# Output rows of two heads of a gated linear attention layer: transposed by DMA in 16-bit words instead of by TensorE

## The chip, the cores and the metric

The kernel runs on one core of a Trainium2 chip, in one launch. The metric is the device time of one execution in microseconds (us). The engines are TensorE (PE in the profile; its weight loads are PEld), VectorE (DVE), ScalarE (ACT), GpSimd (POOL), and SyncE (SP), which here does nothing but issue DMAs. ACT also issues some DMAs on a queue of its own.

## The reference

Two layers run over 528 tokens, 16 learned meta tokens and 512 others: first gated linear attention (GLA) with four heads, then differential softmax attention, with a root mean square norm before each and one at the end. The change is in the first. Its core, cut:

```python
def gla_branch(xn, w_in, w_gate_up, b_gate, gnorm, w_out):      # xn: 528 x 1024
    q, k, v, z, g_lr = split(xn @ w_in)                          # four heads: q, k 256 wide, v, z 512 wide
    lg = log_sigmoid(g_lr @ w_gate_up + b_gate) / 16
    ...                                                          # o = causal, decayed linear attention of q, k, v
    o = o * rsqrt(mean(o * o, axis=-1) + 1e-6) * gnorm           # for each head and token, over 512 values
    y = silu(z) * o
    return y @ w_out
```

Everything is float32, and the kernel keeps nearly that precision: each operand of a product is split into a rounded high part and a remainder (fp32r), and the product is made of three.

## The kernel before

**Layout.** Channels lie on the 128 partitions and tokens in the free dimension, for the projections and for z. Within a head the tokens are cut into block 0 (the 16 meta tokens) and blocks 1 to 4 of 128 each (`BLK`). The output o of a block comes out of TensorE with tokens on the partitions, 128 x 512, since the norm runs over a token's 512 values; y is wanted with channels on the partitions, 4 x 128 channels by tokens, as operand of the output projection. So every block's output has to be turned.

**The steps round the change.** `gla_blocks` (L1194) runs once a head. For each block `output` makes o in a PSUM tile `ps` (L371 are its products), ACT squares it and sums the squares (L1215), DVE and POOL make the reciprocal root (L512, L513), and ACT copies o, scaled by it, to an SBUF tile `t` (L1217), taken from five buffers (`tmp`). `rows` of a block is called after the fill that follows `output`: TensorE transposes the four 128 x 128 pieces by products with an identity (L1239), DVE multiplies them by z out of PSUM (L1241), and `split` makes the high part on ACT (L269) and the remainder on DVE (L270). The rows of block b-1 stand just ahead of the output of block b, those of block 4 at the end.

**What sets the order.** TensorE's program is in the order in which the code is written. Between the steps of a head, `W.fill(us)` draws products from queued generators: projections of the following head and the output projection of the head before. They go through three kinds of PSUM bank, bx, by and bv (L402), each of them in groups of four or eight products of 264 columns, whose results ACT and DVE take up in partial sums (ACT copies one bank to `u` at L423, DVE adds at L448). `fill=(1.9, 1.6)` are the microseconds of such products ahead of and behind each block; block 0 has 0.6 ahead. ACT, DVE, POOL and SP get their order from a scheduler, in which the steps marked `@urgent` go ahead of others. Behind `gla_blocks` the generators are run dry (`W.finish`), and the next head begins with its z, its scores, and `gla_cross` for four blocks (products at L1176, copies of them to `cm` on ACT, L378 and L379, called from `gla_ready`) beside the value projection of the head after it. The output projection of a head (products at L938) runs in the next head's stretch.

**Weights and queues.** Weight halves are loaded by SP into `raw` (two buffers), ACT makes the high part `wh` (L269), DVE the remainder `wl` (L270); for sums of two weights DVE adds first (L337). A generator asks for the next one when it has used one up. SP's queue also carries, late in each head, a conditional copy of scores (`steep`, L1160).

**Turning by DMA** exists for the values of heads 1 and 2 (and of the second layer): `turn_by_dma` (L549) has ACT copy a 32-bit tile so that the low and high 16-bit words of each number lie apart (L560, 128 x 1056 words to `keep`), writes it to DRAM on ACT's queue (L561), and reads it back on SP's by a transposing DMA of 16-bit words (L569), which puts the words together again with rows and columns changed. `W.follow(steps)` queues steps that come when so many microseconds of products have been drawn, `behind` holds transposing DMAs until SP has issued its next weight load, and `W.land()`, ahead of `gla_blocks`, makes sure that all is done. Head 3 makes its values by TensorE during head 2.

Of the kernel before, what the change touches and what calls it, by code (L numbers as in the profile page):

```python
# [20 lines left out]
P = 128  # L21
# [52 lines left out]
class Weaver:  # L74
# [17 lines left out]

    def follow(self, *steps):

        self.away.append([steps[0][0], list(steps)])

    def onward(self, us=0.0):
        for d in list(self.away):
            d[0] -= us
            while d[0] <= 0:  # L100
                d[1].pop(0)[1]()
                if not d[1]:
                    self.away.remove(d)
                    break
                d[0] += d[1][0][0]

    def land(self):

        while self.away or self.behind:
            self.onward(1000.0)  # L110
            while self.behind:
                self.behind.pop(0)()

# [95 lines left out]
def trunk(ctx, tc, x, meta, g_norm, gla_w_in, gla_w_gate_up, gla_b_gate, gla_gnorm, gla_w_out,  # L209
# [21 lines left out]
    def T(p, shape, dt, tag, **kw):  # L231
        uid[0] += 1
        return p.tile(shape, dt, tag=tag, name=f"{tag}_{uid[0]}", **kw)
# [58 lines left out]
    def load(key):  # L292
        t = load_w(*key) if len(key) == 4 else load_blocks(*key)
        while behind:
            behind.pop(0)()
        return t
# [252 lines left out]
    def turn_by_dma(planes, groups, ends, us, done, last):  # L549
# [7 lines left out]
        @urgent  # L557
        def leave(m, src):
            pl = words(planes[:, m, :]).rearrange("p (h c) -> p h c", h=2)
            act.activation(pl, words(src).rearrange("p (c h) -> p h c", h=2), AF.Copy)  # L560
            act.dma_start(vd[m], pl)  # L561
            left.remove(m)
            if not left:
                W.follow((4.0, lambda: behind.append(turn)))

# [359 lines left out]
    def q_gla_out(hd, s, sink=None):  # L925
# [3 lines left out]
        def gen():  # L929
            turns[0] = 0  # L930
            for c in range(4):
                h = ws.take()
# [260 lines left out]

    def gla_blocks(hd, s, fill, last):  # L1194

# [6 lines left out]
        def output(b):  # L1202
# [14 lines left out]
            act.activation(on[:n], po[:n], AF.Copy, scale=st[:n, 1:2])  # L1217
            return on

        def take_y():  # L1220
# [24 lines left out]

        prev = None
        for b in range(5):
            W.fill(fill[0] if b else 0.6)
            if prev is not None:
                rows(b - 1, prev)  # L1250
            prev = output(b)
            W.fill(fill[1])
        W.fill(2.0)
        rows(4, prev)

# [17 lines left out]
    for hd in range(G_HEADS):  # L1273
# [32 lines left out]
        W.land()  # L1306
        gla_blocks(hd, s, (1.2, 1.2) if last else (1.9, 1.6), last)
        W.finish()
# [575 lines left out]
```

## Time and profile before

| | before |
|---|---|
| three runs: median (lowest to highest) | 986.19 us (986.02 to 986.84) |
| the profiled execution, its time | 986.58 us |
| its span in the trace | 984.8 us |
| TensorE busy | 969.7 us, 98% |
| DVE, ACT, POOL busy | 777.3, 615.6, 50.7 us |
| TensorE clock granted, mean | 0.997 of full speed |
| the two stretches of `gla_blocks` of heads 1 and 2 | from 212 and 316 us on |

The span runs from the first to the last instruction in the trace, and the execution's time has some 2 us round it. In the profile each group of instructions has its line, engine, operation, and its tiles as out<-in. A row of a timeline gives the start, the length in us, engine, line, operation, tiles, shapes and how many alike follow each other, with the idle time before it and what released it in brackets. Lengths of TensorE's instructions are modelled and overlap; distances between starts do not. Groups are made of instructions of one line; L402, for instance, is the line of all projection products.

### The profile page before, as it was taken

Reading aid. Unit: us, or ns where it says so; the run is one execution under the profiler, and the core shown is the slowest. Engines: PE = TensorE matmul, PEld = TensorE weight load, DVE = VectorE, ACT = ScalarE, POOL = GpSimd, SP = SyncE. Lnnn points to the kernel's source line nnn. Section 1 sums busy time; section 2 is a strip of 40 time slices with the busy share of each in tenths; the row PEclk is TensorE's granted clock in tenths of the full one; section 3 lists DMA queues with packets and bytes.
Section 4 is the critical chain, followed back from the end, with each engine's and each line's share of the span. In section 5 each row is a group of like instructions: output and inputs, shape, how many; then the busy total and the mean of one; then the engine's idle time right before and its main releaser. Section 6 shows DMA issues by size and latency. Waiting matters only on the chain. (4 is left out here: it accounts for less than half of the span.)

```text
span 984.8 us, 18186 instructions
## 1 busy us (share of the span) xinstructions
PE 969.7 (98%) x7065; PEld 915.2 (93%) x7065; DVE 777.3 (79%) x1584; ACT 615.6 (63%) x1306; POOL 50.7 (5%) x68
## 2 busy tenths in 40 slices
PE   8999999999999999999999999999999999999997
PEld 8999999999999999999999998898998999988896
DVE  7889985987687888556998885877968879677785
ACT  7776755566546666536657675566764667654583
POOL 1000000000000100000000101001010000000001
PEclk9999999999999999999999999999999999999999
DMA  7322223731363322122332524335353351622222
GB/s 194 87 74 74 74 87 127 143 87 44 111 158 87 86 73 76 68 86 87 97 87 77 149 63 137 83 98 135 86 147 86 97 135 49 184 60 81 86 65 86
DMA packets 150474, 96.27 MB, mean 98 GB/s; under 512 B 33117, under 2 KB 136829, under 8 KB 150384
## 3 DMA queue, kind: packets, MB, share of 16 engines
q1 hardware_dynamic: 147504, 89.61, 33.5%
q10 hardware_dynamic: 2880, 5.46, 1.6%
q8 instruction: 57, 0.93, 0.4%
q14 instruction: 33, 0.27, 0.1%
HBM read 83.64 MB, written 7.57 MB: 93 GB/s over the span
## 5 line engine op out<-in xcount | busy, mean ns | idle before, releaser
L270 DVE TENSOR_TENSOR wl<-raw,wh 128x1024 fp32r<-128x1024 f32 x98 | 119.6, 1222 | 26.9 <-ACT wh L269 19.9
L269 ACT ACTIVATE wh<-raw 128x1024 fp32r<-128x1024 f32 x98 | 103.0, 1053 | 52.2 <-PE by L938 26.6
L402 PE MATMUL bv<-x,wh 128*128 128x264 f32 (+1 forms) x656 | 97.7, 287 | 0.8 <-DVE t L448 0.6
L402 PE MATMUL bx<-x,wh 128*128 128x264 f32 (+1 forms) x640 | 95.1, 286 | 0.2
L402 PEld LDWEIGHTS bv<-x,wh 128*128 128x128 f32 x656 | 86.3, 189 | 1.8 <-DVE t L448 1.5
L402 PEld LDWEIGHTS bx<-x,wh 128*128 128x128 f32 x640 | 84.6, 188 | 1.4 <-ACT u L423 0.6
L392 PE MATMUL bx<-x,wh 128*128 128x512 f32 (+1 forms) x256 | 62.5, 386 | 0.0
L423 ACT ACTIVATE u<-bx 128x264 f32<-128x264 f32 (+1 forms) x120 | 45.4, 379 | 24.1 <-PE bx L402 21.9
L270 DVE TENSOR_TENSOR wl<-sum,wh 128x1024 fp32r<-128x1024 f32 x41 | 50.1, 1221 | 11.0 <-ACT wh L269 9.7
L1618 ACT ACTIVATE p<-p,st 128x528 f32<-128x528 f32 (+3 forms) x64 | 36.4, 569 | 31.7 <-DVE st L1616 31.4
L402 PE MATMUL bv<-x,wl 128*128 128x264 f32 (+1 forms) x328 | 55.2, 285 | 0.1
L1654 POOL TENSOR_TENSOR st<-st,mhalf 128x1 f32<-128x1 f32 x32 | 30.6, 957 | 466.4 <-ACT on L1652 422.8
L402 PE MATMUL bx<-x,wl 128*128 128x264 f32 (+1 forms) x320 | 53.8, 285 | 0.0
L392 PEld LDWEIGHTS bx<-x,wh 128*128 128x128 f32 x256 | 44.5, 188 | 8.0
L269 ACT ACTIVATE wh<-sum 128x1024 fp32r<-128x1024 f32 x41 | 43.3, 1055 | 10.7 <-PE bv L402 4.0
L269 ACT ACTIVATE a11h<-raw 128x512 fp32r<-128x512 f32 x41 | 25.7, 628 | 35.5 <-DMA raw<-in_diff_w_in_dram 18.0
L402 PE MATMUL by<-x,a12h 128*128 128x264 f32 (+1 forms) x320 | 46.7, 286 | 0.2 <-DVE t L448 0.2
L402 PE MATMUL bx<-x,a11h 128*128 128x264 f32 (+1 forms) x320 | 46.5, 285 | 0.0
L402 PEld LDWEIGHTS bv<-x,wl 128*128 128x128 f32 x328 | 45.9, 188 | 0.4 <-issue 0.3
L402 PEld LDWEIGHTS bx<-x,wl 128*128 128x128 f32 x320 | 45.0, 188 | 0.5 <-DVE wl L270 0.2
L402 PEld LDWEIGHTS bx<-x,a11h 128*128 128x128 f32 x320 | 42.3, 188 | 0.8
L402 PEld LDWEIGHTS by<-x,a12h 128*128 128x128 f32 x320 | 41.7, 188 | 0.6 <-DVE t L448 0.4
(479 smaller groups left out, 2644.2 us busy)
## 6 DMA issues: line engine op xcount, KB each, us to landing
raw<-in_gla_w_in_dram SPq DMA_DIRECT2D x48, 512.0 KB, 4.2
raw<-in_diff_w_in_dram SPq DMA_DIRECT2D x42, 512.0 KB, 5.6
raw<-in_diff_w_in_dram SPq DMA_DIRECT2D x11, 1024.0 KB, 5.7
raw<-in_gla_w_out_dram SPq DMA_DIRECT2D x8, 1024.0 KB, 5.3
raw<-in_diff_w_out_dram SPq DMA_DIRECT2D x8, 1024.0 KB
vd<-planes ACTq DMA_DIRECT2D x12, 268.0 KB, 3.0
vd<-keep ACTq DMA_DIRECT2D x8, 264.0 KB, 2.3
T<-bdr SPq DMA_DIRECT2D x8, 264.0 KB, 3.6
```

The lines of the kernel that those rows point to most:

```text
L269: act.activation(hi, src, AF.Copy)
L270: dve.tensor_tensor(lo, src, hi.bitcast(F32), op=ALU.subtract)
L392: pe.matmul(bank, a[:, k, :], b[k] if n0 is None else b[k][:, n0 + i * nn:n0 + (i + 1) * nn], start=n == 0 and ks[0] == 0, stop=n == len(t ...
L402: pe.matmul(bank[:, :x[q].shape[2]], w[p][:, k * P:(k + 1) * P], x[q][:, k, :], start=first and i == 0, stop=i == len(PASSES) - 1, skip_gr ...
L423: W.moved = act.activation(t, self.bx[:, :self.n], AF.Copy, scale=self.sc)
L1618: act.activation(p[:, :nk], p[:, :nk], AF.Exp, scale=-1.0, bias=st[:, m:m + 1], accum_out=st[:, 2 + m:3 + m])
L1654: pool.tensor_tensor(ms, ms, mhalf[:, :1], op=ALU.pow)
```

## The change

For heads 1 and 2 (`far`) the outputs of blocks 1 to 4 are turned by transposing DMAs in place of TensorE. For each block ACT copies the scaled output, words of its numbers apart, to a tile of its own (128 x 1024 words) and starts the write to DRAM on its queue. After each pair of blocks, (1, 2) and (3, 4), one transposing DMA on SP's queue (issued behind the next weight load, or at the latest when the head's output projection begins) brings both back into the first four of the eight rows of `b_all`, an SBUF buffer of the gates that is free then and takes the word copies of the next head's values after, with channels on the partitions. `scaled_rows` of each block follows 11.0 and 1.5 us of drawn products later: the multiply by z in DVE, now in SBUF and in place, and `split` as before. Block 0 keeps TensorE. `fill` becomes (0.6, 1.2) in these heads, the fill of 2.0 and the rows behind block 4 are gone, and `W.land(s)` at the start of the head's output projection makes the queued steps of that head come. Heads 0 and 3 are as before.

```diff
--- before.py
+++ after.py
@@ -90,12 +90,12 @@
     def defer(self, us, fn):
         self.late.append([us, fn])
 
-    def follow(self, *steps):
-
-        self.away.append([steps[0][0], list(steps)])
-
-    def onward(self, us=0.0):
-        for d in list(self.away):
+    def follow(self, *steps, tag=None):
+
+        self.away.append([steps[0][0], list(steps), tag])
+
+    def onward(self, us=0.0, tag=None):
+        for d in [d for d in self.away if tag in (None, d[2])]:
             d[0] -= us
             while d[0] <= 0:
                 d[1].pop(0)[1]()
@@ -104,12 +104,13 @@
                     break
                 d[0] += d[1][0][0]
 
-    def land(self):
-
-        while self.away or self.behind:
-            self.onward(1000.0)
-            while self.behind:
-                self.behind.pop(0)()
+    def land(self, tag=None):
+
+        while any(tag in (None, d[-1]) for d in self.away + self.behind):
+            self.onward(1000.0, tag)
+            for d in [d for d in self.behind if tag in (None, d[-1])]:
+                self.behind.remove(d)
+                d[0]()
 
     def spent(self, us):
         self.onward(us)
@@ -292,7 +293,7 @@
     def load(key):
         t = load_w(*key) if len(key) == 4 else load_blocks(*key)
         while behind:
-            behind.pop(0)()
+            behind.pop(0)[0]()
         return t
 
     def w_pair(shape):
@@ -561,7 +562,7 @@
             act.dma_start(vd[m], pl)
             left.remove(m)
             if not left:
-                W.follow((4.0, lambda: behind.append(turn)))
+                W.follow((4.0, lambda: behind.append((turn, None))))
 
         def turn():
             for blocks, c0 in groups:
@@ -928,6 +929,7 @@
 
         def gen():
             turns[0] = 0
+            W.land(s)
             for c in range(4):
                 h = ws.take()
                 for mm in range(2):
@@ -1191,7 +1193,7 @@
             gla_cross(hd, s, b)
             W.fill(1.5)
 
-    def gla_blocks(hd, s, fill, last):
+    def gla_blocks(hd, s, fill, last, far):
 
         s.y = None
 
@@ -1217,6 +1219,37 @@
             act.activation(on[:n], po[:n], AF.Copy, scale=st[:n, 1:2])
             return on
 
+        def far_rows(pair):
+
+            yd = T(dp, [2, P, 2, 512], U16, "yd", bufs=2)
+            src = yd.rearrange("m p h c -> (m p h) c")
+            i = pair[0] - 1
+            raw = b_all[:, i:i + 2, :].rearrange("p m c -> p (m c)")[:, :8 * P].rearrange("p (m c) -> p m c", m=4)
+            left = [0, 1]
+
+            @urgent
+            def leave(j, on):
+                pl = words(tmp()[:, :512]).rearrange("p (h c) -> p h c", h=2)
+                act.activation(pl, words(on).rearrange("p (c h) -> p h c", h=2), AF.Copy)
+                act.dma_start(yd[j], pl)
+                left.remove(j)
+                if not left:
+                    W.follow((4.0, lambda: behind.append((turn, s))), tag=s)
+
+            def turn():
+                tc.keep_in_program_order(sp.dma_start(words(raw), src, transpose=True))
+                W.follow((11.0, lambda: scaled_rows(0)), (1.5, lambda: scaled_rows(1)), tag=s)
+
+            def scaled_rows(j):
+                t0, n = BLK[pair[j]]
+                y = raw[:, :, j * P:(j + 1) * P]
+                with tc.issue_after(W.mark.ins):
+                    dve.tensor_tensor(y, y, s.z[:, :, t0:t0 + n], op=ALU.mult)
+                    for m0, m1, hi, lo in s.groups:
+                        split(hi[:, :, t0:t0 + n], lo[:, :, t0:t0 + n], y[:, m0:m1, :])
+
+            return leave
+
         def take_y():
 
             if not last:
@@ -1243,15 +1276,20 @@
             for m0, m1, hi, lo in s.groups:
                 split(hi[:, :, t0:t0 + n], lo[:, :, t0:t0 + n], y[:, m0:m1, :n])
 
-        prev = None
+        prev, leave = None, None
         for b in range(5):
             W.fill(fill[0] if b else 0.6)
-            if prev is not None:
+            if prev is not None and (b == 1 or not far):
                 rows(b - 1, prev)
             prev = output(b)
+            if far and b:
+                if b % 2:
+                    leave = far_rows((b, b + 1))
+                leave(1 - b % 2, prev)
             W.fill(fill[1])
-        W.fill(2.0)
-        rows(4, prev)
+        if not far:
+            W.fill(2.0)
+            rows(4, prev)
 
     W.fill(5.0)
     pf = ps_tile()
@@ -1304,7 +1342,8 @@
         else:
             W.stop = q_gla_v(hd + 1, heads[hd + 1])
         W.land()
-        gla_blocks(hd, s, (1.2, 1.2) if last else (1.9, 1.6), last)
+        far = hd in (1, 2)
+        gla_blocks(hd, s, (1.2, 1.2) if last else (0.6, 1.2) if far else (1.9, 1.6), last, far)
         W.finish()
         W.stop = None
 
```

Three pieces of the engines' orders follow, before and after. Numbers behind names tell tiles apart and shift between the two versions, as lines do by one to five behind the edits (to L1217) and by more behind `far_rows` (the transposes are L1272 in place of L1239).

TensorE in `gla_blocks` of head 1, ahead of and at block 1's output; by, bv and bx are banks of the projection that fills, ident,t the transposes of the 16 meta rows, and ps_5617 and ps_5588 the output of block 1. Before:

```order
L402 MATMUL by_5564<-x_2_78,a12l_5455 128x264 x4
L402 MATMUL bv_5582<-x_4_80,wh_5450 128x264 x8
L402 MATMUL bv_5582<-x_4_80,wl_5451 128x264 x4
L402 MATMUL bx_5473<-x_752_3925,wh_5519 128x264 x3
L1239 MATMUL ps_5608<-ident,t_5550 128x16 x4
L371 MATMUL ps_5617<-v_885_4661,a_905_4759 128x512
```

After:

```order
L403 MATMUL by_5564<-x_2_78,a12h_5454 128x264 x8
L403 MATMUL by_5564<-x_2_78,a12l_5455 128x264 x4
L1272 MATMUL ps_5579<-ident,t_5550 128x16 x4
L372 MATMUL ps_5588<-v_885_4661,a_905_4759 128x512
L372 MATMUL ps_5588<-v_886_4662,a_905_4759 128x512
```

Eight, four and three products that stood ahead of the meta rows' transposes are behind block 1's output now.

ACT in the stretch of head 1 in which head 2's values are projected beside `gla_cross`; raw_5716 and raw_5758 are the same weight and wh_6072 and wh_6058 its high part, keep_83 the word copies of head 2's values that the kernel had before, cm copies of cross products, of which those from ps_6117 before and ps_6103 after belong to block 2. Before:

```order
L269 ACTIVATE a_1110_5986<-t_5998 128x512
L560 ACTIVATE keep_83<-t_5960 128x1056
L269 ACTIVATE wh_6072<-raw_5716 128x1024
L561 DMA vd_5540<-keep_83 128x1056
L560 ACTIVATE keep_83<-t_5959 128x1056
L378 ACTIVATE cm_6088<-ps_6091 32x128
```

After:

```order
L379 ACTIVATE cm_6074<-ps_6077 32x128
L562 DMA vd_5540<-keep_83 128x1056
L380 ACTIVATE cm_6074<-ps_6077 32x128
L424 ACTIVATE u_6094<-bx_6014 128x264
L379 ACTIVATE cm_6074<-ps_6103 32x128
L380 ACTIVATE cm_6074<-ps_6103 32x128
L270 ACTIVATE wh_6058<-raw_5758 128x1024
```

The high part stood ahead of all cm copies and stands behind those of blocks 1 and 2 now.

DVE in the same stretch of head 2, where head 3's values are projected and TensorE turns them itself; t_7235 and t_7210 are value columns, sum_7360 the sum for a weight that is used later, keep_83,z the multiply by z of the rows that came back by DMA, and y their remainder. Before:

```order
L270 TENSOR_TENSOR a11l_7357<-raw_7228,a11h_7356 128x512
L337 TENSOR_TENSOR sum_7360<-raw_7228 128x512
L337 TENSOR_TENSOR sum_7360<-sum_7360,raw_7228 128x512
L381 TENSOR_TENSOR am_7269<-t_7273,am_7269 32x16
L448 SCALAR_TENSOR_TENSOR t_7235<-by_7318,u_7300 128x264
```

After:

```order
L1247 TENSOR_TENSOR keep_83<-keep_83,z_6546 128x4x128
L449 SCALAR_TENSOR_TENSOR t_7210<-bv_7212,u_7278 128x264
L271 TENSOR_TENSOR y_1237_6844<-keep_83,y_1236_6843 128x4x128 x2
L271 TENSOR_TENSOR wl_7229<-sum_7163,wh_7228 128x1024
L449 SCALAR_TENSOR_TENSOR t_7210<-by_7296,u_7278 128x264
```

The sum and the remainder a11l that stood ahead of the value columns are further down now, and the multiply of the turned rows and their remainders stand there.

## The prediction

> **What bounds the kernel now.** I read the busy table of the page first, then the waits, then TensorE's instructions in order of time round the edited stretch, then what ACT, DVE, POOL and SP do in it.
>
> ```profile
> span 984.8 us, 18186 instructions
> PE 969.7 (98%) x7065; PEld 915.2 (93%) x7065; DVE 777.3 (79%) x1584; ACT 615.6 (63%) x1306; POOL 50.7 (5%) x68
> PE ps L1239 <- ACT t L1217: 1.1, 4, 0.3
> ```
>
> TensorE (PE) is busy for 98% of the span, so an instruction taken off it shortens the run by its own length, unless a wait comes in its place. The transposes that the change removes (L1239) already wait for the scaled rows that ACT writes at L1217, 1.1 us in four waits. The stretch of head 1 where they stand, in TensorE's timeline (start, length, what, and in brackets idle time before it and its releaser):
>
> ```profile
> 212.05 0.41 PE L402 MATMUL bx<-x,wh 128*128 128x264 f32 x2
> 214.45 1.14 PE L402 MATMUL bv<-x,wh 128*128 128x264 f32 x8
> 215.42 0.65 PE L402 MATMUL bv<-x,wl 128*128 128x264 f32 x4
> 216.65 0.41 PE L1239 MATMUL ps<-ident,t 16*128 16x16 f32 x4 [0.22 <-ACT t L1217]
> 217.00 0.97 PE L371 MATMUL ps<-v,a 128*128 128x512 f32 x3
> 228.33 0.66 PE L1239 MATMUL ps<-ident,t 128*128 128x128 f32 x4
> 228.75 0.94 PE L371 MATMUL ps<-v,a 128*128 128x512 f32 x3
> 241.85 0.65 PE L402 MATMUL bv<-x,wl 128*128 128x264 f32 x4
> 242.85 0.66 PE L1239 MATMUL ps<-ident,t 128*128 128x128 f32 x4 [0.35 <-ACT t L1217]
> 346.09 0.65 PE L402 MATMUL bv<-x,wl 128*128 128x264 f32 x4
> 347.04 0.66 PE L1239 MATMUL ps<-ident,t 128*128 128x128 f32 x4 [0.31 <-ACT t L1217]
> ```
>
> Lengths are modelled and overlap; cost is the distance between starts. Eight products take 215.42 - 214.45 = 0.97 us, 0.121 each. Four transposes take 228.75 - 228.33 = 0.42 us. The last two rows are the same place in head 2, 104 us later.
>
> **Term 1, removed.** Two heads, four blocks, four transposes: 8 x 0.42 = -3.3 us. With them go the waits ahead of each head's last block. Four products after 241.85 end at 242.34, the transposes start at 242.85: 0.51 us; in head 2, 347.04 - 346.58 = 0.46. Together -1.0 us. What stands behind the transposes is neutral: multiply by z, ACT's copy and DVE's remainder are still done once per block, later and from SBUF.
>
> **Term 2, a wait that grows.** The 16 meta rows keep their transposes, but the fill ahead of them shrinks: in the first pair of order pieces in the section on the change, fifteen projection products (eight with wh, four with wl, three of the next bank) that stood ahead of them now stand behind block 1. What the transposes wait for cannot come earlier:
>
> ```profile
> 214.36 0.57 ACT L1215 ACTIVATE t<-ps 16x512 f32<-16x512 f32 x1
> 215.35 0.54 POOL L513 TENSOR_TENSOR st<-st,mhalf 16x1 f32<-16x1 f32 x1 [79.87 <-DVE st L512]
> 215.92 0.68 ACT L1217 ACTIVATE t<-ps,st 16x512 f32<-16x512 f32 x1
> 320.86 0.42 PE L1239 MATMUL ps<-ident,t 16*128 16x16 f32 x4 [0.21 <-ACT t L1217]
> ```
>
> Square, POOL's power and scaling copy are queued behind the same instructions as before on ACT, DVE and POOL, so the meta rows still start at 216.65, while PE is through at 214.45: 2.2 us of idle (0.2 of it old), in head 2 the same. Block 1 starts when it did, and the fifteen products are still to be done: 15 x 0.121 = 1.8 us a head, +3.6 us. Bounds: nothing, if that chain came 2.2 us earlier, for which no order gives a reason; and all of it. I take all.
>
> **Term 3, a weight split that comes late.** In head 1 the value projection of head 2 runs beside gla_cross. By the second pair of order pieces the split of its weight half, wh_6058, which stood ahead of every cm copy, now stands on ACT behind those of block 2 (ps_6103). They need PE's cross products, and PE wants the weight six products after these.
>
> ```profile
> 256.62 1.04 ACT L269 ACTIVATE wh<-raw 128x1024 fp32r<-128x1024 f32 x1
> 257.69 1.23 DVE L270 TENSOR_TENSOR wl<-raw,wh 128x1024 fp32r<-128x1024 f32 x1 [0.59 <-ACT wh L269]
> 260.07 1.14 PE L402 MATMUL bx<-x,wh 128*128 128x264 f32 x8
> 262.42 0.61 PE L402 MATMUL bx<-x,wl 128*128 128x264 f32 x3
> 262.70 0.27 ACT L378 ACTIVATE cm<-ps 32x128 fp32r<-32x128 f32 x1 [1.29 <-PE ps L1176]
> ```
>
> Before, the weight was there 2.4 us early. Now, from the last cross product: ACT answers 0.28 us later (262.70 against 262.42 for block 3), two cm copies 0.57, split 1.04, about 0.1 to PE: 2.0 us, against 6 x 0.121 = 0.73. PE waits 1.3 us, then its remainder wl (1.23 us on DVE behind wh) is 0.4 us later than eight products: +1.7 us. Bounds: 0, if ACT and PE keep another distance than their orders say, and 1.7. I take 1.6. In head 2 the corresponding split stands five us ahead of its use.
>
> **Term 4, waits that go in head 2.** There PE turns values itself and lost time to a late DVE:
>
> ```profile
> 360.02 0.69 DVE L337 TENSOR_TENSOR sum<-raw 128x512 f32<-128x512 f32 x1 [0.60 <-DMA raw<-in_gla_w_in_dram]
> 361.67 0.43 DVE L448 SCALAR_TENSOR_TENSOR t<-by,u 128x264 f32<-128x264 f32 x1
> 361.43 0.65 PE L402 MATMUL bx<-x,wl 128*128 128x264 f32 x4
> 362.15 0.66 PE L833 MATMUL ps<-ident,t 128*128 128x128 f32 x4
> 363.84 1.16 PE L1176 MATMUL ps<-qs,kd 128*128 128x128 f32 x8 [0.19 <-DVE kd L1180]
> 366.75 0.28 PE L834 MATMUL ps<-ident,t 128*32 128x128 f32 x1 [0.59 <-DVE v L270]
> ```
>
> By starts PE lost about 0.2, 0.4 and 0.8 us. In the third pair of order pieces the value columns t that PE turns stood on DVE behind the sum of a weight whose load was late (0.60 from DMA, above); now they stand behind the moved multiply and its remainders, and the sum comes later. I count -1.2 us, between 0 (the moved work delays DVE by what the load did) and -1.4.
>
> **What is added at no cost.** Eight 16-bit copies on ACT, eight writes on its queue, four transposing transfers on SP's. The first row has the four copies of this sort that the kernel makes for head 2's values; the next is the transposing transfer of their first half, with SP's time in it. Rows of windows give the stretch, its length, busy time (and count) of PE, PEld, DVE, ACT and POOL, clock, the DMA engines' share and GB/s.
>
> ```profile
> L560 ACT ACTIVATE keep<-t x4: 1065/1068/1085, 255.6 to 270.6; 128x1056 uint16<-128x1056 uint16 x4
> 273.19 4.96 SPq L569 DMA_TRANSPOSE keep<-vd  x1
> 280.00:282.00 2.00, 2.00 (x18) 2.00 (x18) 2.00 (x5) 1.06 (x1) 0.00 (x0) 1.00 0.36 61
> 282.00:284.00 2.00, 2.00 (x19) 2.00 (x18) 2.00 (x5) 1.65 (x3) 0.00 (x0) 1.00 0.00 0
> 249.52 0.37 SPq L278 DMA_DIRECT2D raw<-in_gla_w_out_dram  x1
> 252.49 0.09 SPq L1160 DMA_DIRECT2D t<-steep  x1
> 269.03 0.40 PE L938 MATMUL bx<-y,wh 128*128 128x264 f32 x2
> 212.00:244.00 32.00, 31.43 (x223) 29.04 (x223) 25.38 (x48) 20.46 (x42) 3.56 (x5) 1.00 0.24 67
> raw<-in_gla_w_in_dram SPq DMA_DIRECT2D x48, 512.0 KB, 4.2
> ```
>
> A copy is 1.07 x 1024/1056 = 1.04 us, 4.2 us a head, where ACT was busy 20.5 of 32 us. A transfer of this shape holds SP about 5 us, and the engines' share is zero 9 us after its issue. The second of head 1 goes behind the out-projection load (249.52, now some 3 us earlier), lands by about 256, and the rows are wanted at 269.03: cover of over 10 us. The steep copy behind it would be issued near 252, as before. Without that cover each us late is a us of PE.
>
> The Trainium skill (VectorE: DVE Perf Modes, "Rules for kernel authors") advises TensorE for a 128x128 transpose when PSUM will do as destination, and it did here. Its table ("The three transpose paths") has 390 ns against 1309 ns for 16-bit data; by the trace one takes 0.105 us on PE, and a transfer in place of eight holds SP for 5 us: the trace agrees on the side, more sharply. Had anything to wait for such a transfer, that rule would make this change a loss of some us a head; its length counts only there.
>
> **Sum.** -3.3 - 1.0 + 3.6 + 1.6 - 1.2 = -0.3 us, on a span of 984.8: 984.5. Span and time of the profiled execution differ by 986.58 - 984.80 = 1.8 us, and its time is 0.4 above the median of the three runs, 986.19. That is 1.4 us above the span: the run is forecast at 985.9, no change: below 0.2%, 2.0 us, a measurement of this kernel cannot tell from nothing.
>
> **Rivals.** *Faster, 984:* the late split does not bite, term 3 is nil: -3.3 - 1.0 + 3.6 - 1.4 = -2.1, 984.1. For it: ACT had idle time all over the stretch. Against: the order puts the copy of block 2's cross products ahead. Much lower it cannot go while the meta rows wait. Chance 0.20.
>
> *Slower, 989:* ACT becomes the bound between the blocks.
>
> ```profile
> 218.75 0.57 ACT L1215 ACTIVATE t<-ps 128x512 f32<-128x512 f32 x1
> 221.35 0.69 ACT L1217 ACTIVATE t<-ps,st 128x512 f32<-128x512 f32 x1 [1.61 <-POOL st L513]
> ```
>
> From 216.7 to 232.7, between meta rows and block 4's end, its order has four squares (0.57) and scaling copies (0.69), four 16-bit copies (1.04), and five or six weight splits (1.04 at L269) with partial sums: 9.2 us, 5 to 6 and a little, about 15 of 16 us, in order, with four power chains in them at which it may wait as for the 1.61 us here. PE next needs the partial sum u (L423's copy of a bank) of the following unit near 237.0; adding these lengths up in ACT's order I place it at 236.3 to 236.7. From 0.7 us of slip on, each us on ACT is one on PE; if every block slips by 0.5 that is 2 less 0.5, 1.5 us a head, 3 in all: 989. Against: before, ACT left 11 us of 32 unused here. Chance 0.28.
>
> *Slower, 989, by SP's queue:* a transposing transfer that waits for its write holds up the steep copy and weights behind it; 3 us late, less 1.5 of cover, is 1.5 a head, 989. Against: the queue keeps up (4.2 us in the median from issue to landing of a weight load, last row above). Chance 0.07.
>
> That the rows are still turned by PE is out: 32 identity products are gone from its order.
>
> **How the numbers follow.** Forecast, no change, 0.45; its own range 984.5 to 987.5. Faster 0.20 is the chance of below 984.2; the two slower rivals make 0.35. Range 984.0 to 989.4.
>
> **What would show it.** Meta rows' transposes (L1272) with 2 us of idle ahead, from ACT, in heads 1 and 2; no L1239-like groups of 128x128; about 1.5 us of wait for wh in bx of head 1's value projection, and none for values in head 2's; the moved multiply (L1247) waiting for no transfer. Wrong would be waits for partial sums or weights between the blocks, or a meta-row wait under 1 us.

## The result: 2.1 us slower, and the profile after

| | before | changed |
|---|---|---|
| median of ten runs each | 986.11 us | 988.20 us |
| lowest to highest | 985.59 to 986.88 | 986.54 to 991.14 |
| ratio to before, 95% interval | | 1.0023 (1.0013 to 1.0034) |
| the profiled execution: time, span | 986.58, 984.8 us | 990.28, 988.2 us |

The forecast was no change at 985.9 us. The time lies inside its range, but the change is a loss that the measurement can tell from nothing: the interval excludes 1, though the prediction held that 2.0 us could not be told from none. The profiled execution is 2.1 us above the median of its kernel, so its losses are larger than those of a typical run; the next paragraphs come back to that.

The busy table of the changed kernel, and its waits on TensorE (PE), each with total us, number and longest:

```profile
span 988.2 us, 18164 instructions
PE 967.4 (98%) x7033; PEld 913.5 (92%) x7033; DVE 776.7 (79%) x1584; ACT 626.6 (63%) x1314; POOL 50.3 (5%) x68
PE ps L1272 <- ACT t L1219: 3.8, 2, 2.0
PE ps L372 <- DVE aT L271: 2.0, 2, 1.3
PE ps L1700 <- ACT on L1694: 1.2, 1, 1.2
PE bx L403 <- ACT wh L270: 1.0, 1, 1.0
```

TensorE has 32 instructions less and is busy for 2.3 us less, yet the span is 3.4 us longer. Two of the waits are those that the prediction named (for the scaled meta rows, and for `wh`). The other two, L372 and L1700, lie in layer 2, in code that the change does not touch; before they were 0.7 and 0.3 us.

The place of the meta rows in head 1, in TensorE's timeline of the changed kernel, and the same row in head 2:

```profile
213.31 0.65 PE L403 MATMUL by<-x,a12l 128*128 128x264 f32 x4
215.98 0.41 PE L1272 MATMUL ps<-ident,t 16*128 16x16 f32 x4 [2.02 <-ACT t L1219]
...
217.47 1.96 PE L403 MATMUL bv<-x,wh 128*128 128x264 f32 x8
219.22 1.08 PE L403 MATMUL bv<-x,wl 128*128 128x264 f32 x4
...
322.76 0.42 PE L1272 MATMUL ps<-ident,t 16*128 16x16 f32 x4 [1.76 <-ACT t L1219]
```

The idle time is there, as forecast. What was not forecast stands behind it: eight products take 219.22 - 217.47 = 1.75 us by their starts, where eight of the same sort took 0.97 before. The table of windows (columns as in the prediction; the clock is the third number from the end) tells why:

```profile
214.00:215.00 1.00, 0.00 (x0) 0.00 (x0) 0.38 (x2) 1.00 (x4) 0.33 (x1) 1.00 0.00 0
217.00:218.00 1.00, 1.00 (x6) 0.85 (x5) 1.00 (x4) 0.37 (x2) 0.00 (x0) 0.61 1.15 338
218.00:219.00 1.00, 1.00 (x6) 1.00 (x6) 0.82 (x4) 0.54 (x3) 0.23 (x1) 0.50 1.15 289
219.00:220.00 1.00, 1.00 (x6) 1.00 (x6) 0.00 (x0) 0.54 (x1) 0.32 (x1) 0.50 0.25 59
220.00:221.00 1.00, 1.00 (x8) 1.00 (x7) 0.45 (x1) 1.00 (x2) 0.00 (x0) 0.68 0.03 8
```

After the idle time TensorE is granted half its clock for 3.41 us, which costs 0.39 + 0.50 + 0.50 + 0.32 = 1.71 us of full clock. The same stretch comes in head 2. Before, no such stretch lies in these heads. Nothing in the list of waits shows this loss: an instruction at half clock is busy, not waiting. The mean granted clock of each of the ten runs bears it out: the three at 0.995 took 989.96 to 991.14 us, the seven at 0.997 to 0.999 took 986.54 to 988.51.

The difference of the spans by stages, from the starts of the same TensorE instructions in both traces:

| stage | changed less before |
|---|---|
| start of the program, ahead of the changed code | -0.67 us |
| head 1, blocks | +0.81 |
| head 1, value projection of head 2 (term 3) | +1.48 |
| output projection of head 1, in head 2's stretch | +0.66 |
| head 2, blocks | +0.42 |
| head 2, turning of values (term 4) | -1.06 |
| layer 2 | +1.80 |
| sum | +3.44 |

A tenth or so moves between neighbouring stages with the instruction at which one is cut from the next.

In layer 2 two waits grew, each behind a weight load. Here is one of them in both kernels: SP's issue of the load, then VectorE's wait for it. First before, then changed:

```profile
897.09 0.99 SPq L285 DMA_DIRECT2D raw<-in_diff_w_in_dram  x2
903.10 0.69 DVE L337 TENSOR_TENSOR sum<-raw 128x512 f32<-128x512 f32 x1 [3.39 <-DMA raw<-in_diff_w_in_dram]
```

```profile
899.21 0.99 SPq L286 DMA_DIRECT2D raw<-in_diff_w_in_dram  x2
906.56 0.69 DVE L338 TENSOR_TENSOR sum<-raw 128x512 f32<-128x512 f32 x1 [4.73 <-DMA raw<-in_diff_w_in_dram]
910.45 0.73 PE L372 MATMUL ps<-v,aT 128*128 128x256 f32 x4 [1.31 <-DVE aT L271]
```

From issue to use it is 6.01 us before and 7.35 in the changed kernel; the add that is late by 1.3 us makes VectorE's `aT` late, and TensorE waits 1.31 us for it. The view of DMA queues for the window from the issue to about the landing (packets, MB, share of 16 engines), before and then changed:

```profile
q1 hardware_dynamic: 2153, 1.20, 77.8%
```

```profile
q1 hardware_dynamic: 2212, 1.30, 68.2%
q8 instruction: 1, 0.02, 0.8%
```

In the changed kernel one packet of another queue is among the load's: a 16 KB piece of program code. It holds one of the DMA engines for 0.9 us in the midst of the load. Half of the load's 2048 packets are through 3.4 to 3.5 us after the issue in both kernels; the last comes after 5.4 us before, and after 6.8 in the changed one.

### The profile page after: what moved, and what is told of

Read it like the earlier page. It is cut to its first block, busy times and chain, and to the rows that moved or that the text cites. A ratio compares the mean times of both kernels' runs of the same rounds, so it can differ in the third digit from the quotient of the medians.

```text
span 988.2 us, 18164 instructions
## 1 busy us (share of the span) xinstructions
PE 967.4 (98%) x7033; PEld 913.5 (92%) x7033; DVE 776.7 (79%) x1584; ACT 626.6 (63%) x1314; POOL 50.3 (5%) x68
```

## The experiments

Two theories stood after the comparison. For the heads: the idle time ahead of the meta rows costs the products that are not done in it, and a half-clock stretch besides. For layer 2: either the four new DRAM tiles `yd` shift other data to worse places (the placement theory, P in the expectations), or the 32 products and 32 weight loads fewer on TensorE shift the points at which its code is fetched. In all, TensorE's queue runs 14130 instructions of both sorts before, and the page lists 57 packets on the instruction queue: a piece per 248 instructions, by which this queue is read as TensorE's code. So 64 fewer should move each later fetch by 64/14130 of the run, 4.5 us (an estimate), against the loads beside it. In the trace the 53rd piece comes at 892.3 us before and at 901.9 in the changed kernel, which is 2.1 us late by then: 7.5 us later against its work, and into the load above. The results are ratios to runs of the kernel before on the same chip, with 95% intervals.

**The fill given back** (the change as it is, with the old fill ahead of the meta rows; the fills behind make up for it):

```diff
-            W.fill(fill[0] if b else 0.6)
+            W.fill((1.9 if far and b == 1 else 0.0 if far and b == 2 else fill[0]) if b else 0.6)
...
-            W.fill(fill[1])
+            W.fill((1.6, 0.0)[b] if far and b < 2 else fill[1])
```

> The changed kernel, with the products that it draws between blocks 1 and 2 drawn ahead of the meta rows' transposes again. Theory (idle time and clock): the 2.0 and 1.8 us in which TensorE waits for the meta rows go, 15 x 0.121 = 1.8 us a head, and with them the two stretches of 3.41 us at half clock that follow them in the changed kernel's trace, up to 1.7 us each. No clock below 1 in the middle of the program, 988.2 - 3.6 - 1.7 to 3.4 = 981 to 983, and a spread of single times near that of the kernel before (1.3 us) in place of 4.6. Rival 1 (the clock has nothing to do with the idle time): 984.6 at best, half-clock stretches and spread stay. Rival 2 (ACT becomes the bound once blocks 1 and 2 stand close): waits for partial sums between the blocks, 986 or more.

Measured: 985.85 us against 985.63, ratio 0.9997 (0.9988 to 1.0006), no change. TensorE's timeline at the meta rows of head 1:

```profile
215.75 0.53 PE L403 MATMUL bx<-x,wh 128*128 128x264 f32 x3
216.32 0.42 PE L1272 MATMUL ps<-ident,t 16*128 16x16 f32 x4
216.67 0.97 PE L372 MATMUL ps<-v,a 128*128 128x512 f32 x3
```

No wait, and the granted clock is 1.00 throughout 214 to 221 us. The stretches of the blocks became 2.1 and 2.2 us shorter than before, which is term 1 by itself. The whole, though, misses the expected 981 to 983 by 3 us or more. The wait for `wh` stays (1.1 us). In head 2 TensorE now waits 1.3 us for a value part `c`, which takes term 4's gain (the stage gains 0.1). And layer 2's late loads stay; this load came as late as in the change, and in the profiled execution the wait behind it brought a half-clock step of its own, from 908.4 us on:

```profile
902.80 0.69 DVE L338 TENSOR_TENSOR sum<-raw 128x512 f32<-128x512 f32 x1 [4.81 <-DMA raw<-in_diff_w_in_dram]
```

```profile
909.00:910.00 1.00, 1.00 (x7) 1.00 (x6) 1.00 (x3) 0.37 (x2) 0.50 (x1) 0.50 0.00 0
```

So the meta-row wait is one cause, and what happens in layer 2 is another that does not hang on it.

**The gap alone** (the kernel before, transposes and all, with the short fill ahead of the meta rows):

```diff
-            W.fill(fill[0] if b else 0.6)
+            W.fill((0.6 if hd in (1, 2) and b == 1 else fill[0]) if b else 0.6)
...
-            W.fill(fill[1])
+            W.fill(1.2 if hd in (1, 2) and b == 0 else fill[1])
```

> The kernel before, with TensorE's transposes, but with the fills round block 0 of heads 1 and 2 cut as the change cuts them, and nothing else. Theory: the meta rows are waited for 2 us in both heads; 3.6 us for products that are not hidden any more, and up to 1.7 us of half clock behind each: 986.1 + 3.6 + 1.7 to 3.4 = 991 to 993, with the half-clock stretches in the trace and a spread of several us. Rival 1 (idle time alone, no clock): 989.7, spread as before. Rival 2 (the wait is made up for later, since the products drawn later fill other waits): 987 or less.

Measured: 990.06 us against 985.63, ratio 1.0047 (1.0032 to 1.0062). Its wait, the window behind it and the load of layer 2:

```profile
PE ps L1239 <- ACT t L1217: 4.0, 2, 2.0
```

```profile
217.00:218.00 1.00, 1.00 (x3) 0.81 (x4) 0.92 (x2) 0.57 (x2) 0.00 (x0) 0.50 1.11 318
```

```profile
906.77 0.69 DVE L337 TENSOR_TENSOR sum<-raw 128x512 f32<-128x512 f32 x1 [3.40 <-DMA raw<-in_diff_w_in_dram]
```

The gap makes the half-clock stretch in both heads without any of the change's DMAs, and costs 2.4 and 2.6 us a head in the trace. The time by itself would not decide: it is a little under the expectation (991 to 993) and nearer to rival 1 (989.7). The old waits ahead of each last block vanish with the gap, and the half-clock windows rule out that rival, as does the spread of 5.0 us. Layer 2 is as before, the load with it: here the number of TensorE's instructions is unchanged.

**The split early** (the change, with the `cm` copies of blocks 1 and 2 told to come behind the high part of the weight):

```diff
-        split3(s.cm[:, cs], pm, 64)
+        with tc.issue_after(W.outer.ins) if hd == 2 and b < 3 else ExitStack():
+            split3(s.cm[:, cs], pm, 64)
```

(`W.outer` is the ACT instruction that makes that high part; the lines that record it are left out here.)

> The changed kernel with one edit: on ACT the high part of the weight half that TensorE waits for beside gla_cross stands ahead of the copies of cross products of blocks 1 and 2. Theory (term 3 is a real loss): TensorE's wait of 1.0 us there falls to 0.2 to 0.4, and the time by 0.6 to 1.2 us: 987.0 to 987.6. Rival (the wait has slack behind it, and TensorE then waits for something else in the same stretch): no change, 988.2 within 0.5. The half-clock stretches stay as in the changed kernel, since nothing ahead of the meta rows is touched.

Measured: 987.81 us against 985.63, ratio 1.0018 (1.0009 to 1.0027). The wait for `wh` is gone: in the first of these two pieces of TensorE's timeline (the changed kernel) its eight products start 1.64 us after the four `wl` products ahead, in the second (this kernel) 0.49 us after them.

```profile
259.64 0.65 PE L403 MATMUL bv<-x,wl 128*128 128x264 f32 x4
261.28 1.25 PE L403 MATMUL bx<-x,wh 128*128 128x264 f32 x8 [0.99 <-ACT wh L270]
262.54 0.39 PE L403 MATMUL bx<-x,wl 128*128 128x264 f32 x1
```

```profile
259.72 0.65 PE L404 MATMUL bv<-x,wl 128*128 128x264 f32 x4
260.21 1.14 PE L404 MATMUL bx<-x,wh 128*128 128x264 f32 x8
261.22 0.39 PE L404 MATMUL bx<-x,wl 128*128 128x264 f32 x1
```

The stage lost 0.1 us instead of 1.5. Term 3 was rightly caused by ACT's order; in the median (987.81, between the ranges of theory and rival) it is hardly to be seen beside the spread of these runs (985.80 to 990.00). That spread goes with the clock: the four runs at 0.993 and 0.994 took 988.93 to 990.00 us, the six at 0.997 took 985.80 to 987.95.

**Gaps by themselves.** A kernel that leaves the whole computation out and has TensorE do equal products in trains, with waits of growing length for ACT between them:

```python
GAPS = [(k, r) for r in range(3) for k in range(0, 3200, 160)]
...
    for n, (k, r) in enumerate(GAPS):
        for g in range(11 + (n * 7) % 5):
            ps = ps_pool.tile([P, 512], F32, tag="ps", name=f"ps_{n}_{g}")
            for i in range(8):
                pe.matmul(ps[:, :264], w, wide[:, :264], start=i == 0, stop=i == 7)
        act.activation(wide[:, :264], ps[:, :264], AF.Copy, scale=1.0e-3)
        if k:
            act.activation(wide[:, 264:264 + k], hold.rearrange("p b c -> p (b c)")[:, :k], AF.Copy)
            act.activation(wide[:, :264], hold.rearrange("p b c -> p (b c)")[:, k:k + 264], AF.Copy)
```

> No part of the reference: 60 stretches of 88 to 120 equal products of 264 columns on TensorE, with a wait for ACT behind each whose length goes in steps from about 0.6 to about 5 us, three times over. It leaves out the whole computation and copies x to the output. Theory: the granted clock goes to half in steps of 3.41 us, for a step that follows a step in which TensorE was idle for about half of its time or more; a wait of about 1.8 us does it where it falls into one step, and one of 2.5 us where it is cut by the boundary of two does not always. Rival 1: only a step without any work does it, so no wait below 3.4 us lowers the clock. Rival 2: any wait above a fixed length does it, wherever it falls.

Two of its waits, of nearly one length, and a window behind each (PE, PEld, ACT, POOL, clock, DMA share, GB/s):

```profile
144.71 13.71 PE L38 MATMUL ps<-wide,w 128*128 128x264 f32 x112 [2.01 <-ACT wide L42]
443.05 13.45 PE L38 MATMUL ps<-wide,w 128*128 128x264 f32 x96 [1.87 <-ACT wide L42]
```

```profile
145.00:146.00 1.00, 1.00 (x10) 1.00 (x10) 0.00 (x0) 0.00 (x0) 1.00 0.00 0
444.00:445.00 1.00, 1.00 (x7) 1.00 (x6) 0.00 (x0) 0.00 (x0) 0.50 0.00 0
```

The longer one cost nothing, behind the shorter one the clock was halved. All clock changes in this trace lie on a grid of steps of 3.413 us, and the grid lies elsewhere in the program in each profiled execution. What counts is TensorE's idle time within one step: of the steps with 1.71 us or less (66) none was followed by a half-clock step, but for one of 0.64 us that followed a half-clock step itself; with 1.74 to 1.84 us one of five was; with 1.87 and more (23) every one. A wait of 2.94 us that a boundary cut into 1.46 and 1.48 did nothing. So both rivals are out. The edge is that of this kernel of equal products; among the tuned kernel's mixed instructions it lay lower. Steps with 1.54 us of idle time by the trace (fill given back, behind the late load), 1.62 (the old tile, below) and 1.76 (the change, head 2) were followed by half clock; those with up to 1.38 were not.

So the meta-row waits, 2.02 and 1.76 us, sit near the edge: whether they cost half a step, 3.413/2 = 1.7 us, depends on where the grid happens to lie. A wait of 2.0 us has 1.8 of it in one step for (3.41 - 2.0 + 0.4)/3.41 = 0.53 of the positions, one of 1.8 us for 0.47: 1.7 us a run in the mean, up to 3.4. With an edge of 1.55 it is 0.68 and 0.61, 2.2 us; both are estimates. That fits the changed kernel's spread of 4.6 us where the kernel before has 1.3, with the granted clocks of the single runs above, and explains why the profiled execution, with both stretches, is above its median.

**Placement** was tested from both sides. The kernel before with the four DRAM tiles, and a write of 32 bytes to each:

```diff
+            if hd in (1, 2) and b in (1, 3):
+                yd = T(dp, [2, P, 2, 512], U16, "yd", bufs=2)
+                act.dma_start(yd[0, 0:1, 0, :16], prev.bitcast(U16)[0:1, :16])
```

> The kernel before, with the four DRAM tiles of 512 KB that the change adds, but only 32 bytes written into each by one small DMA on ACT's queue, and nothing else. In the changed kernel the transposing transfers of values behind the edit hold SP longer (5.4 and 6.0 us in place of 5.0 and 4.5 near 274 and 287; 3.9 in place of 2.6 near 674) and loads land later in both layers, by which TensorE loses some 2.5 us. Theory P (placement: the new tiles move the addresses of all later tiles of values in DRAM, by 1 and 2 MB): this kernel shows the same longer transfers and late loads, without any of the change's work: 987.5 to 988.5. Rival T (the added transfers themselves do it): the transfers of values as in the kernel before and 985.6 to 986.2. Rival N (noise of the profiled executions): the same.

And the change with its rows in a part of an existing DRAM tile:

```diff
-            yd = T(dp, [2, P, 2, 512], U16, "yd", bufs=2)
+            n = ((hd - 1) * 2 + pair[0] // 2) * 262144
+            yd = words(hT_dr.rearrange("p k l -> (p k l)"))[n:n + 262144].rearrange("(m p h c) -> m p h c", m=2, p=P, h=2)
```

> The changed kernel with the words of the rows put into a DRAM tile that it has anyway and that is free then, so that every later tile has its address of the kernel before. Theory P: the transfers of values take 5.0 and 4.5 us near 274 and 287 and 2.6 near 674 again, the waits for loads in head 1's output projection and in layer 2 go: 988.0 less 2 to 2.5, 985.5 to 986. Rival T or N: 987.5 to 988.5, no difference to the changed kernel. The waits for the meta rows and the half-clock stretches stay in either case.

Measured: 985.66 us for the first, ratio 1.0002 (0.9994 to 1.0011), and 988.60 for the second, 1.0029 (1.0018 to 1.0040), both against 985.58. Tiles without the change cost nothing, and the change without tiles costs as much as with them. The placement theory is out; rival T, the added transfers themselves, is not settled by these two.

**The three edits together** (fill given back, split early, rows in the existing tile, each as in its diff above):

> The changed kernel with three edits at once: the products between blocks 1 and 2 drawn ahead of the meta rows (first experiment), the weight split ahead of the cross products' copies (third), and the words of the rows in the DRAM tile that is there anyway (the edit beside this one). If the three losses are separate and theory P holds: 988.0 - 2.1 - 0.4 - 2.3 = 983.2, faster than the kernel before by 2.5 us. If theory P falls: 985.4. Rival (the gain of one is lost at the next wait): 985.5 or more though theory P holds alone.

Measured: 984.09 us against 985.58, ratio 0.9985 (0.9977 to 0.9994): 1.5 us faster than the kernel before, and 1.3 less than the sum for a false theory P, so that sum had a loss too small. Layer 2's load is late still:

```profile
898.54 0.69 DVE L338 TENSOR_TENSOR sum<-raw 128x512 f32<-128x512 f32 x1 [4.41 <-DMA raw<-in_diff_w_in_dram]
```

**The gap filled with empty products** (the change, with eight small products ahead of the meta rows of both heads; the trace counts each as two, so that 32 products and as many weight loads are back):

```diff
+            if far:
+                for _ in range(8):
+                    pe.matmul(pt[:, P:2 * P], ones, ones, start=True, stop=True)
```

> The changed kernel with eight useless products of 128x128 (the ones that warm TensorE at the program's start) ahead of the meta rows' transposes in heads 1 and 2, in time in which it waits; nothing else changes. They are 32 TensorE instructions a head with their weight loads, 64 in all, as many as the removed transposes were. Theory (clock): the idle time is filled, so no half-clock stretches, -1.7 us on average. Theory F (code loading): TensorE's own instructions arrive by DMA in pieces of 16 KB, one per 256 of them; 64 fewer instructions move each piece by some us, in the changed kernel into weight loads (near 674 and 902), whose last packets then come 1.0 to 1.5 us later; with 64 back the pieces fall as in the kernel before, and the waits near 682 and 907 lose their 2 us together. Both: 988.1 - 1.7 - 1.5 = 984.9. Clock alone: 986.4, with the late loads still there. Rival: 988 as before, since the wait itself (1.8 us a head) stays.

Measured: 985.53 us against 986.11, ratio 0.9997 (0.9988 to 1.0006), between the forecasts for both effects (984.9) and for the clock alone (986.4). Nothing useful is done in the gap, it is only not idle. Its timeline, the window behind, and the load:

```profile
213.41 1.95 PE L1273 MATMUL ps<-ones 128*128 128x128 f32 x16
215.51 0.42 PE L1275 MATMUL ps<-ident,t 16*128 16x16 f32 x4 [0.15 <-ACT t L1219]
```

```profile
218.00:219.00 1.00, 1.00 (x11) 1.00 (x10) 0.45 (x3) 0.43 (x2) 0.23 (x1) 1.00 0.75 201
```

```profile
901.52 0.69 DVE L338 TENSOR_TENSOR sum<-raw 128x512 f32<-128x512 f32 x1 [3.40 <-DMA raw<-in_diff_w_in_dram]
```

The block stretches are now 0.7 and 0.6 us shorter than before. With the fill given back they were 2.1 and 2.2 shorter, so the lost products are worth 1.4 to 1.6 us a head; the changed kernel's blocks are 1.5 and 1.0 longer than these, which is the clock. And since the number of instructions is back, the load of layer 2 is in time, with no code packet in its window, though all the change's transfers are there: that puts out rival T. The spread is back to 1.6 us.

**The number of instructions put back at the start** (the three edits together, and small products among those that warm TensorE up; the three edits' lines are left out here):

```diff
-    warm_up(10)
+    warm_up(6)
+    for _ in range(20):
+        pe.matmul(warm[:32, :32], ones[:, :32], ones[:, :32], start=True, stop=True)
```

> The kernel with the three edits (984.1 measured), and the warming products at the start of the program cut to six and followed by twenty small ones of 32x32, so that TensorE has 64 instructions more from the start; nothing else. Theory F: behind head 2 the pieces of TensorE's code are loaded at the same instructions as in the kernel before, the loads near 665 and 895 are in time again and the waits there fall by 1.8 us; the pieces in layer 1 ahead of head 1 move by 64 the other way and may hit other loads; some 0.5 us more at the start: 982.8. Rival: 984.1 to 984.6, waits in layer 2 as before.

Measured: 982.67 us against 986.11, ratio 0.9969 (0.9957 to 0.9981), the fastest version, 3.4 us better than the kernel before. Its interval overlaps a little with that of the three edits (from 0.9977), so the step between the two rests on the trace. The load is in time:

```profile
897.00 0.69 DVE L338 TENSOR_TENSOR sum<-raw 128x512 f32<-128x512 f32 x1 [3.46 <-DMA raw<-in_diff_w_in_dram]
```

**The number of instructions taken away alone** (the kernel before, without `warm_up(10)` and two later `warm_up(3)`: 32 products and 32 weight loads fewer, and nothing of the change):

```diff
-    warm_up(10)
...
-    warm_up(3)
+    pass
...
-    warm_up(3)
+    pass
```

> The kernel before without 16 of its warming products at the start, that is with 64 TensorE instructions less, and nothing of the change. Theory F: the late loads of the changed kernel near 674 and 897, and TensorE's waits behind them (1.2 in place of 0.3 us, 2.0 in place of 0.7), appear here too: +1.5 us in layer 2, beside what the colder start costs (its first 20 us are compared by themselves). Rival: layer 2 takes as long as in the kernel before, to 0.3 us.

Measured: 992.23 us against 986.11, ratio 1.0065 (1.0051 to 1.0078). This number says little, since the start of the program is changed and waits 5.6 us for x in the profiled execution, itself the fastest of six at 987.13. What tells is its trace from head 2 on. Behind the blocks of head 2 it is 2.1 us ahead of the kernel before, late in layer 2 it is 0.5 us behind. Its load and the queues in that load's window:

```profile
903.62 0.69 DVE L337 TENSOR_TENSOR sum<-raw 128x512 f32<-128x512 f32 x1 [4.66 <-DMA raw<-in_diff_w_in_dram]
```

```profile
q1 hardware_dynamic: 2216, 1.30, 66.0%
q8 instruction: 1, 0.02, 0.9%
```

With none of the change's DMAs, tiles or waits, 64 instructions fewer bring the code packet into the load, and 2.6 us are lost between these two places, 0.8 and 1.3 of them at the two late loads. In the profiled kernels that keep TensorE's number (before, gap alone, tiles alone, gap filled, put back) the last packet of this load comes 5.3 to 5.5 us after its issue, and in those that lack 64 (the change, fill back, split early, rows in the old tile, the three edits, this one) after 6.4 to 7.0.

## Why the prediction failed, step by step

**Term 1** (transposes removed, with their waits, -2.15 us a head) held: -2.1 and -2.2 with the fill given back.

**Term 2 failed.** Its cause was right: the meta rows waited 2.02 and 1.76 us where 2.2 was foretold, for the copy at L1219. Its price counted the fifteen products alone (1.8 us a head; 1.4 to 1.6 measured). The step that the prediction left out is that TensorE's clock reacts to idle time: 3.41 us at half clock behind each wait cost 1.5 and 1.0 us more in the trace. The gap alone shows it without the change, and the filled gap shows the change without it. The prediction priced every product at the full clock of its rows from before, and put two idle times of 2 us into them.

The Trainium skill (TensorE: Matmul & The Clock Gate, "Part 1: The HAM clock gate") gives a free-running window of 3413 ns, and the trace agrees with 3.413 us. The same page ("HAM oscillation — how this bites in real kernels") has as its rule that no idle gap may be over about 3.4 us. By it the waits here, 2.0 us, would be harmless; measured, 1.87 us within a step was enough each time in the kernel of gaps, and 1.54 us once in the tuned one.

**Term 3** (+1.6) measured +1.48: a wait of 0.99 us for `wh`, where 1.3 was expected, and then `wl` later than the eight products, which stretch to 262.54 - 261.28 = 1.26 us for 0.97. In the changed kernel ACT has the weight's split behind block 2's `cm` copies:

```profile
259.60 0.27 ACT L379 ACTIVATE cm<-ps 32x128 fp32r<-32x128 f32 x1
259.88 0.27 ACT L380 ACTIVATE cm<-ps 32x128 fp32r<-32x128 f32 x1
260.17 1.06 ACT L270 ACTIVATE wh<-raw 128x1024 fp32r<-128x1024 f32 x1
```

**Term 4** (-1.2) measured -1.06: in the changed kernel the values' transposes no longer wait. **The free additions** were free: none of the eight moved multiplies waits for a transfer (the first is shown), and no wait of TensorE on a partial sum of ACT came up between the blocks.

```profile
249.99 0.67 DVE L1247 TENSOR_TENSOR keep<-keep,z 128x512 f32<-128x512 f32 x1
```

So neither the rival by ACT's load nor that by SP's queue happened, though the time came near theirs; that it lies inside the stated range is luck. The faster rival failed with the split being late.

**What no step had:** late loads through code fetches. Layer 2 lost 1.80 us in the trace, where the prediction has nothing behind head 2; that loads come late by the number of TensorE's instructions is shown by the two kernels that change only that (taken away alone, and put back against the three edits). The output projection of head 1 lost 0.66 us in the same manner, by the trace. The queue of code in the window of a pair of weight loads there (286.4 to 293.9 us), which had no packet before:

```profile
q8 instruction: 1, 0.02, 1.0%
```

The fetch comes at 290.6 us there, 4.2 us behind the loads' issue. The stage loses 0.7 to 1.2 us in the four profiled kernels with the fetch 4 to 5 us behind (the change, fill back, split early, old tile), and nothing where it comes ahead of the loads or 10 us behind them (gap filled, three edits, put back). But in the kernel with instructions taken away alone it comes 4.2 us behind and costs nothing. So this place is read, not shown.

Put together from the measured terms: -4.3 for the transposes, +3.0 for the idle products, +1.5 and -1.1 for terms 3 and 4 make -0.9, and the filled-gap version, which has these and neither of the surprises, came to -0.6 in its medians. The prediction's sum was -0.3, so its terms were near enough; what it lacked decided. The clock (2.6 us in the trace) and the stages with late loads (2.5) turned that into +3.4 in the profiled execution, which was 0.7 us ahead at the start (its cause was not followed up), and +2.1 in the median.

**Left open:** the three-edits version and the best one still spread over 3.9 and 3.5 us without any meta-row wait, and no run tells why; the granted clock does not, since it was 0.998 or 0.999 in the fastest and the slowest runs of both. The best version gained 3.4 us in the median where the terms left to it (-4.3, +0.4, -1.1) make 5.0. Of the difference its trace shows 0.9: with the fill given back term 4's gain goes, since TensorE waits in head 2 for the value part `c`:

```profile
PE ps L838 <- DVE c L271: 1.3, 1, 1.3
```

The rest stays open.

## What to carry to other kernels

When an edit puts an idle time of about 1.5 us or more on a TensorE that runs through, price the clock behind it too (here 1.7 us, in half to two thirds of the positions by estimate) and, if no useful work can be put there, try empty products. When the number of TensorE's instructions changes, look again at every load that is used as soon as it lands, far from the edit too: compare the instruction queue's packets in their windows, and put the number back by some small products to tell this effect from the edit itself. Judge such an edit by a version with both effects taken out, since its own worth may be hidden by them: here the same idea was 2.1 us slower as written and 3.4 faster with its fill, one copy's order and its instruction count mended (its rows moved to another tile too, which by itself gained nothing).

## What the runs showed of the hardware that was not expected

- In the kernel of gaps the granted clock changes only on a grid of 3.413 us. About half a step of idle time within one step (1.87 us always, 1.71 never) halves the clock of the next; a wait of 2.94 us cut by a boundary did nothing. In the tuned kernel 1.54 us was enough once, and 1.38 not.
- A 16 KB code packet in the midst of a 2048-packet load holds one DMA engine for 0.9 us, and the last packets of the load come 1.0 to 1.6 us later, though the median packet does not. The Trainium skill (Runtime: NRT & Kernel Launch, "Instruction fetch mechanics") has the refill in blocks of 16 KiB or 256 instructions, with which the 248 by the page agree, and calls its cost mostly hidden; in the changed kernel's trace no wait of TensorE is put down to its own code, but it waited 1.31 us for what hung on the load that the code had delayed.
